# Layer A's channel-major products: high and low half of the input as one 512-column operand, and their sums joined ahead of the convolution

## The chip, the cores and the metric

The kernel runs on one core of one Trainium2 chip, in one launch. The metric is the device time of that launch in microseconds, as the median of several runs. Before the change it is 1284.6 us, the median of 3 runs from 1283.5 to 1285.86.

## What is computed

The reference is a decoder trunk of two layers on 256 rows of 2048 channels, in float32. Only layer A matters here. Its mixer multiplies the modulated input `h` by one wide weight matrix, and puts a causal convolution of width 4 along the sequence on the part that holds x, B and C:

```python
h = x * (1.0 + scale) + shift
proj = h @ in_w
z, xBC, dt = jnp.split(proj, [SSD_D_INNER, SSD_D_INNER + SSD_CONV_DIM], axis=-1)
xBC = jax.nn.silu(_causal_depthwise_conv(xBC, conv_w, conv_b))
xs, Bm, Cm = jnp.split(xBC, [SSD_D_INNER, SSD_D_INNER + SSD_BC_DIM], axis=-1)
...
y = _ssd_chunked(xs * dt[..., None], dt * A, Bm, Cm)
...
y = y * jax.nn.silu(z.astype(jnp.float32))
```

A gated norm, an output product, a layer norm, keys and values for all of layer B, and layer B's windowed attention follow.

## The kernel before

**Products in halves.** Each float32 operand of a large product is split into a high half, which float32r holds, and a low half, the rest. A product of two such operands takes three matmuls: high by high, high by low, low by high. The weights come from HBM in pieces of 128 partitions x 1024 float32 (512 KB; `load_piece`, L86, six buffers `raw`), and `split` (L91) makes `whi` on ACT (L94) and `wlo` on DVE (L95, raw minus whi), four buffers each. The input's halves of layer A lie in `hp` (L269): all 16 blocks of the high half, then all 16 of the low half, 256 columns a block. In layer B they lie in `xp` (L702), and there the high and low half of one block are neighbours.

**Two forms of a channel-major product.** In such a product the weights are what TensorE holds, and the input streams past; the result has channels on partitions and the 256 rows as columns. `cm_piece` (L109) issues, for each of 2 blocks of the input and each of 4 blocks of 128 output channels, three matmuls of 256 columns: L119 (`hi` by `ahi`), L120 (`hi` by `alo`) and L121 (`lo` by `ahi`), all into one half of a PSUM bank. `cm_quad` (L133) does a whole product of 512 channels so. `cm_wide` (L140), used in layer B alone, does 256 channels: one matmul of 512 columns (L151: `hi` by both halves of the input, which fills a bank with two sums side by side) and one of 256 (L152: `lo` by `ahi`, onto the first half of the bank). Its two sums are joined behind it by an ACT copy (L156) and a DVE add (L157). Its pieces hold 4 input blocks x 256 channels, where those of `cm_quad` hold 2 blocks x 512 channels; both are 512 KB.

**Layer A.** The program has a head (L351 to L490), in which the input is modulated as its column products arrive, and in which 10 later products are begun with the blocks that are there (`begun`, L292: the part sums lie in `szt` and in `y[0..7]` until needed). Then `product` (L326) is called for each group: `xs` of groups 1 to 7 and `bc` (B and C of two groups) of 2, 4 and 6 are channel-major; `z` is not. Of the channel-major ones `xs` 1 and `bc` 2 have blocks 4 to 15 left (`k0=4`), `bc` 4 and `bc` 6 blocks 12 to 15 (`k0=12`), and the other six all 16. `product` takes `cm_quad`'s two banks as four tiles (`tiles`, L159). Where a part sum exists, two DVE adds of 512 columns put the banks onto it (L344). The convolution (`conv`, L298) then reads each tile four times: an ACT activation (L302) and three DVE operations of 255, 254 and 253 columns (L305), and ACT's SiLU ends it (L307). It reads PSUM where there was no part sum, SBUF where there was one.

**What shares the engines there.** Between the products stand the scores and the scan of each group (`stage1`, `stage2`, `stage3`), and one column product of the gate, a DVE pass over 2048 columns (L236), goes with every fifth piece (`R = (1, 5)`). PSUM has eight banks; in this stage four are `mm` (tiles `acc`), two `aux`, two `aux2`. A pair of `acc` takes two of the four.

**What sets the order.** Nothing is run as it is written: `arrange` (L1316) lists all instructions with their dependencies, prices each (`price`), runs a list scheduling of the whole program six times and fixes the order of every engine's queue by the best. So an edit in one stage can move instructions in another.

Of the kernel before, what the change touches and what calls it, by code (L numbers as in the profile page):

```python
# [19 lines left out]
P = 128  # L20
# [23 lines left out]

CI, CT, CM, NCONST = 0, 128, 256, 512

CD, CA, NBIAS = 0, 256, 256 + 768


@with_exitstack  # L50
def trunk(ctx, tc, xT, x, c, par, cst, bias, lnrow, ada, wdt, win, wout, wkv, wk1, wbin, wbout, out):
    nc = tc.nc
    V, S, T, PO = nc.vector, nc.scalar, nc.tensor, nc.gpsimd

# [85 lines left out]
    def cm_wide(src, dst, rate=(0, 1)):  # L140


        ps = acc_pair()
        for q in range(KT // 4):
            hi, lo = (t.rearrange("p k n -> p (k n)").rearrange("p (k n) -> p k n", k=4)
                      for t in split(load_piece(src[q])))
            for k in range(4):
                kt = 4 * q + k
                for n in range(2):
                    c_ = slice(n * P, n * P + P)  # L150
                    T.matmul(ps[n], hi[:, k, c_], xp[:, kt], start=kt == 0, stop=False, skip_group_check=True)  # L151
                    T.matmul(ps[n][:, 0, :], lo[:, k, c_], xhi[:, kt, :], start=False, stop=kt == KT - 1,  # L152
                             skip_group_check=True)
            background(*rate)
        for n in range(2):
            S.activation(dst[:, n, :], ps[n][:, 1, :], AF.Copy)  # L156
            V.tensor_tensor(dst[:, n, :], ps[n][:, 0, :], dst[:, n, :], op=ALU.add)  # L157
# [108 lines left out]
            jobs.pop(0)()  # L266


    hp = act.tile([P, 2, KT, L], F32R, name="actT")  # L269
    hhi, hlo = hp[:, 0], hp[:, 1]  # L270

    with ExitStack() as cA:
        pa = cA.enter_context(tc.tile_pool(name="pa", bufs=1))
# [13 lines left out]
        with ExitStack() as cS:  # L287
# [38 lines left out]
            def product(kind, g, pre=None):  # L326

                src, k0, part = begun.get((kind, g), (None, 0, None))
                if src is None:
                    src = win[{"bc": g // 2, "xs": 4 + g, "z": 12 + g}[kind]]  # L330
                if kind == "z":
                    ps = tm_chunk(src, hh_, hl_, rate=R, k0=k0, pre=pre)
                    if g not in sz:
                        sz[g] = p0.tile([P, 2, 512], F32, name="sz")
                    for b in range(2):
                        if part is not None:
                            V.tensor_tensor(part[:, b, :], ps[b], part[:, b, :], op=ALU.add)
                        S.activation(sz[g][:, b, :], part[:, b, :] if part is not None else ps[b], AF.Silu)
                    return
                ps = cm_quad(src, hhi, hlo, rate=R, k0=k0)  # L340
                t = tiles(ps)
                if part is not None:
                    for w in range(2):
                        V.tensor_tensor(part[:, 2 * w:2 * w + 2, :], ps[w], part[:, 2 * w:2 * w + 2, :], op=ALU.add)  # L344
# [387 lines left out]
    with ExitStack() as cL:  # L732
        pl = cL.enter_context(tc.tile_pool(name="pl", bufs=3))
        ex = cL.enter_context(tc.tile_pool(name="ex1", bufs=2, space=PSUM))
        ps = [acc_pair(), acc_pair(), acc_pair(ex)]
        cm_quads([(wkv[2 * g], ps[g]) for g in range(NG)], xhi, xlo, pre=ahead)
        for g in range(NG):
            evict_k(0, g, ps[g])

        R = (4, 9)  # L740
        queue(pl, cols1[16:])
        jobs.append(lambda: gate_out(1))
        for g in range(NG):
            for w in range(2):
                cm_wide(wk1[2 * g + w], kk[1][:, g, 2 * w:2 * w + 2, :], rate=R)
# [32 lines left out]
    def queries(hq):  # L778
        qq = pc2.tile([P, 12, L], F32, name="qq").rearrange("p (g i) l -> p g i l", g=NG)
        for g in range(NG):  # L780
            for w in range(2):
                cm_wide(wbin[2 * (2 * g + hq) + w], qq[:, g, 2 * w:2 * w + 2, :])
        return qq

    def attend(hq, qq):
# [37 lines left out]
    def z_gate(hq, qq):  # L823
        for w in range(2):
            z = qq[:, 1, 2 * w:2 * w + 2, :]
            cm_wide(wbin[2 * (6 + hq) + w], z)
            S.activation(z, z, AF.Silu)
        V.tensor_tensor(qq[:, 0], qq[:, 0], qq[:, 1], op=ALU.mult)

# [525 lines left out]
def _layout(x, c, ada_w, ada_b, ln_g, ln_b, a_in_w, a_conv_w, a_conv_b, a_dt_bias,  # L1355
            a_A_log, a_D, a_norm_g, a_out_w, kv_w, b_in_w, b_out_w):
    f = np.float32
    par = np.zeros((P, NPAR), f)

    def put(name, a):  # L1360
        par[:a.shape[0], OFF[name][0]:OFF[name][1]] = a

    ab = ada_b.reshape(2, 3, KT, P)
    put("adab", ab.transpose(3, 0, 2, 1).reshape(P, 96))
    put("convw", a_conv_w[0].T.reshape(48, P, 4).transpose(1, 0, 2).reshape(P, 192))
    put("convb", _cm(a_conv_b[0]))
# [27 lines left out]
    return {  # L1394
        "xT": x[0].T.reshape(KT, P, L).transpose(1, 0, 2), "x": x[0], "c": c, "par": par, "cst": cst, "bias": bias,
        "lnrow": np.stack([ln_g[0], ln_b[0], ln_g[1], ln_b[1]]),
        "ada": ada, "wdt": _dt(dt), "win": win,
        "wout": _pieces(a_out_w[0]), "wkv": _pieces(kv_w), "wbin": _pieces(b_in_w[0], 256, 4),
        "wk1": _pieces(kv_w[:, :3072].reshape(D, 3, 2, 512)[:, :, 1].reshape(D, 1536), 256, 4), "wbout": _pieces(b_out_w[0]),
    }  # L1400
# [21 lines left out]
```

## Time and profile before

| | before |
|---|---|
| median of 3 runs | 1284.6 us (1283.5 to 1285.86) |
| the profiled execution, its own time | 1281.55 us |
| its span, first to last instruction | 1279.8 us |
| mean granted TensorE clock | 0.993 |
| PE busy | 1239.4 us, 97% |
| DVE busy | 1039.2 us, 81% |
| ACT busy | 696.6 us, 54% |
| read from HBM | 331.37 MB |

Matmuls are pipelined: the duration of one (about 285 ns for 256 columns) runs from its issue to its end and overlaps the next, so the sum over PE's groups is far more than its busy time. What a stream of matmuls costs is read from the spacing of their starts, in the timeline.

### The profile page before, as it was taken

What the parts mean: (1) busy time and instruction counts of PE and PEld (TensorE: products, weight loads), DVE (VectorE), ACT (ScalarE), POOL (GpSimd) and SP (SyncE); (2) the same over time, 40 slices, a digit from 0 to 9 for tenths busy, and PEclk for the clock granted to TensorE, in tenths of its full rate; (3) what the DMA queues carried; (4) which work ended last, traced back from release to release, by engine and by line L of the source; (5) the groups of instructions that cost most, each with busy time, mean ns of one, the idle gap of its engine ahead of it and who ended that gap; (6) DMA issues with size and microseconds to landing.
All of it is one profiled execution on the core that took longest, in us unless ns stands there. A gap on an engine that the chain in (4) does not pass through costs nothing.

```text
span 1279.8 us, 19378 instructions
## 1 busy us (share of the span) xinstructions
PE 1239.4 (97%) x7386; PEld 1095.2 (86%) x7386; DVE 1039.2 (81%) x1457; ACT 696.6 (54%) x1027; POOL 33.3 (3%) x20
## 2 busy tenths in 40 slices
PE   6999999999999999999999899999999999999995
PEld 4978999899899999788888699888888888888884
DVE  6999978999998887978895799998745647848778
ACT  4644566868577767764333444444445645444551
POOL 0000000000000000000000135000000000000000
PEclk9999999999999999999999899999999999999998
DMA  9999967887785556578997688999866663453571
GB/s 372 422 422 422 384 216 268 314 276 247 240 300 191 173 159 203 162 258 269 400 376 218 222 315 308 396 420 395 299 191 193 211 185 115 147 183 107 155 266 66
DMA packets 80449, 334.82 MB, mean 262 GB/s; under 512 B 9090, under 2 KB 9314, under 8 KB 67684
## 3 DMA queue, kind: packets, MB, share of 16 engines
q1 hardware_dynamic: 80356, 333.58, 73.5%
q8 instruction: 58, 0.95, 0.3%
q14 instruction: 35, 0.29, 0.1%
HBM read 331.37 MB, written 2.18 MB: 261 GB/s over the span
## 4 chain that ended last, share of the span: by engine, by line
PE 78%; DMA 12%; DVE 7%; ACT 1%; issue 1%; SPq 0%; DVEq 0%; ACTq 0%
PE acc L151 12%; PE acc L174 11%; PE acc L173 11%; PE acc L172 11%; PE acc L152 6%; DMA raw<-in_win 6%; PE acc L119 6%; PE acc L121 6%; PE acc L120 6%; DMA araw<-in_ada 5%; DVE wlo L95 2%; PE py L589 1%; DVE araw L236 1%; PE aux L795 1%; PE po L819 1%
## 5 line engine op out<-in xcount | busy, mean ns | idle before, releaser
L95 DVE TENSOR_TENSOR wlo<-raw,whi 128x1024 fp32r<-128x1024 f32 x395 | 488.9, 1244 | 176.5 <-ACT whi L94 175.2
L94 ACT ACTIVATE whi<-raw 128x1024 fp32r<-128x1024 f32 x395 | 417.1, 1057 | 382.1 <-PE acc L174 178.6
L119 PE MATMUL acc<-actT,whi 128*128 128x256 f32 x960 | 273.6, 288 | 11.8 <-ACT actT L382 7.4
L173 PE MATMUL acc<-wlo,actT 128*128 128x512 f32 x704 | 276.4, 393 | 0.6 <-DVE wlo L95 0.6
L172 PE MATMUL acc<-whi,actT 128*128 128x512 f32 x704 | 274.8, 393 | 1.6 <-ACT whi L94 1.0
L121 PE MATMUL acc<-actT,wlo 128*128 128x256 f32 x960 | 270.5, 285 | 1.4 <-DVE wlo L95 1.4
L120 PE MATMUL acc<-actT,whi 128*128 128x256 f32 x960 | 271.3, 285 | 0.0
L151 PE MATMUL acc<-actT,whi 128*128 128x512 f32 x704 | 251.3, 398 | 0.0
L236 DVE SCALAR_TENSOR_TENSOR araw<-araw,cb__72 128x2048 f32<-128x2048 f32 x96 | 218.4, 2286 | 9.0 <-DMA araw<-in_ada 5.7
L152 PE MATMUL acc<-actT,wlo 128*128 128x256 f32 x704 | 201.8, 287 | 0.6 <-DVE wlo L95 0.6
L119 PEld LDWEIGHTS acc<-actT,whi 128*128 128x128 f32 x960 | 185.2, 194 | 15.7 <-ACT actT L382 9.0
L121 PEld LDWEIGHTS acc<-actT,wlo 128*128 128x128 f32 x960 | 184.0, 193 | 2.3 <-DVE wlo L95 2.0
L120 PEld LDWEIGHTS acc<-actT,whi 128*128 128x128 f32 x960 | 185.1, 193 | 0.3
L174 PE MATMUL acc<-whi,actT 128*128 128x512 f32 x448 | 175.1, 391 | 0.0
L172 PEld LDWEIGHTS acc<-whi,actT 128*128 128x128 f32 x704 | 131.9, 188 | 30.1 <-ACT whi L94 2.8
L151 PEld LDWEIGHTS acc<-actT,whi 128*128 128x128 f32 x704 | 132.2, 188 | 29.2
L173 PEld LDWEIGHTS acc<-wlo,actT 128*128 128x128 f32 x704 | 132.3, 188 | 27.5 <-DVE wlo L95 1.1
L152 PEld LDWEIGHTS acc<-actT,wlo 128*128 128x128 f32 x704 | 133.0, 189 | 1.9 <-DVE wlo L95 1.2
L174 PE MATMUL acc<-whi,ylo 128*128 128x512 f32 x256 | 100.8, 394 | 0.0
L174 PEld LDWEIGHTS acc<-whi,actT 128*128 128x128 f32 x448 | 84.1, 188 | 17.5 <-issue 0.5
L174 PEld LDWEIGHTS acc<-whi,ylo 128*128 128x128 f32 x256 | 48.1, 188 | 9.4
L305 DVE SCALAR_TENSOR_TENSOR cacc<-acc,prm,cacc 128x255 f32<-128x255 f32 (+2 forms) x96 | 43.7, 475 | 2.7 <-ACT cacc L302 2.3
(205 smaller groups left out, 1083.1 us busy)
## 6 DMA issues: line engine op xcount, KB each, us to landing
araw<-in_ada SPq DMA_DIRECT2D x96, 1024.0 KB, 7.2
raw<-in_win SPq DMA_DIRECT2D x160, 512.0 KB, 4.9
raw<-in_wkv SPq DMA_DIRECT2D x72, 512.0 KB, 4.9
raw<-in_wout SPq DMA_DIRECT2D x64, 512.0 KB, 5.6
raw<-in_wbin SPq DMA_DIRECT2D x64, 512.0 KB, 4.0
raw<-in_wk SPq DMA_DIRECT2D x24, 512.0 KB, 6.6
cbc<-cumd SPq DMA_DIRECT2D x16, 512.0 KB, 5.3
raw<-in_wbout SPq DMA_DIRECT2D x16, 512.0 KB, 4.3
```

The lines of the kernel that those rows point to most:

```text
L94: S.activation(hi, raw, AF.Copy)
L95: V.tensor_tensor(lo, raw, hi.bitcast(F32), op=ALU.subtract)
L119: T.matmul(o, hi[:, k, c_], ahi[:, kt, :], start=first, stop=False, skip_group_check=True)
L120: T.matmul(o, hi[:, k, c_], alo[:, kt, :], start=False, stop=False, skip_group_check=True)
L121: T.matmul(o, lo[:, k, c_], ahi[:, kt, :], start=False, stop=kt == k1 - 1, skip_group_check=True)
L151: T.matmul(ps[n], hi[:, k, c_], xp[:, kt], start=kt == 0, stop=False, skip_group_check=True)
L152: T.matmul(ps[n][:, 0, :], lo[:, k, c_], xhi[:, kt, :], start=False, stop=kt == KT - 1, skip_group_check=True)
L172: T.matmul(ps[b], h_, hi[:, k, :], start=kt == k0, stop=False)
L173: T.matmul(ps[b], h_, lo[:, k, :], start=False, stop=False)
L174: T.matmul(ps[b], l_, hi[:, k, :], start=False, stop=kt == k1 - 1)
L236: V.scalar_tensor_tensor(raw, raw, 1.0, cb_, op0=ALU.mult, op1=ALU.mult, accum_out=mod[layer][:, ct, j:j + 1])
L305: V.scalar_tensor_tensor(acc[:, o:], ps[:, :L - o], w[:, j:j + 1], acc[:, o:], op0=ALU.mult, op1=ALU.add)
```

## The change

The input's halves of layer A are laid out as those of layer B, block by block (`hp` becomes blocks x 2 halves x 256). `cm_quad` goes away. `cm_wide` takes its operands as arguments and a first block `k0`, and returns its banks; what stood behind it, the copy and the add of layer B, becomes `cm_join`, which layer B's calls now use. `product` does each of its ten channel-major products as two `cm_wide` of 256 channels, from pieces of a new input `wsub`, which holds the same weights cut as layer B's are (4 blocks x 256 channels). Behind each half, two tiles are made: without a part sum, an ACT copy of the bank's second half into a new SBUF tile `ct` and a DVE add of its first half; with one, two DVE adds of 256 columns onto the part sum. The convolution reads SBUF in every case but group 0, which the head computes as before; `cm_piece` is left to the head and to layer B's first three products.

```diff
-    def cm_quad(src, ahi, alo, rate=(0, 1), k0=0):
+    def cm_wide(src, both, high, rate=(0, 1), k0=0):
+
         ps = acc_pair()
-        for q in range(k0 // 2, KT // 2):
-            cm_piece(src, q, ps, ahi, alo, k0=k0)
-            background(*rate)
-        return ps
...
+        for q in range(k0 // 4, KT // 4):
             hi, lo = (t.rearrange("p k n -> p (k n)").rearrange("p (k n) -> p k n", k=4)
                       for t in split(load_piece(src[q])))
             for k in range(4):
                 kt = 4 * q + k
                 for n in range(2):
                     c_ = slice(n * P, n * P + P)
-                    T.matmul(ps[n], hi[:, k, c_], xp[:, kt], start=kt == 0, stop=False, skip_group_check=True)
-                    T.matmul(ps[n][:, 0, :], lo[:, k, c_], xhi[:, kt, :], start=False, stop=kt == KT - 1,
+                    T.matmul(ps[n], hi[:, k, c_], both[:, kt], start=kt == k0, stop=False, skip_group_check=True)
+                    T.matmul(ps[n][:, 0, :], lo[:, k, c_], high[:, kt, :], start=False, stop=kt == KT - 1,
                              skip_group_check=True)
             background(*rate)
+        return ps
...
-    hp = act.tile([P, 2, KT, L], F32R, name="actT")
-    hhi, hlo = hp[:, 0], hp[:, 1]
+    hp = act.tile([P, KT, 2, L], F32R, name="actT")
+    hhi, hlo = hp[:, :, 0, :], hp[:, :, 1, :]
...
-                ps = cm_quad(src, hhi, hlo, rate=R, k0=k0)
-                t = tiles(ps)
-                if part is not None:
-                    for w in range(2):
-                        V.tensor_tensor(part[:, 2 * w:2 * w + 2, :], ps[w], part[:, 2 * w:2 * w + 2, :], op=ALU.add)
-                    t = [part[:, n, :] for n in range(4)]
+                t = []
+                for w in range(2):
+                    ps = cm_wide(wsub[2 * WSUB.index((kind, g)) + w], hp, hhi, rate=R, k0=k0)
+                    for n in range(2):
+                        if part is None:
+                            t.append(p0.tile([P, L], F32, name="ct", bufs=4))
+                            S.activation(t[-1], ps[n][:, 1, :], AF.Copy)
+                            V.tensor_tensor(t[-1], ps[n][:, 0, :], t[-1], op=ALU.add)
+                        else:
+                            t.append(part[:, 2 * w + n, :])
+                            for i in range(2):
+                                V.tensor_tensor(t[-1], ps[n][:, i, :], t[-1], op=ALU.add)
```

TensorE's queue at the start of the product `xs` of group 2, before (`acc_2673` and `acc_2674` are its two banks):

```order
L119 MATMUL acc_2673<-actT_86,whi_2677 128x256
L120 MATMUL acc_2673<-actT_86,whi_2677 128x256
L121 MATMUL acc_2673<-actT_86,wlo_2678 128x256
L119 MATMUL acc_2674<-actT_86,whi_2677 128x256
L120 MATMUL acc_2674<-actT_86,whi_2677 128x256
```

(The second block of 128 channels, in the same bank as the first, stands between the third and the fourth row.) The same product after the change, where its first half (`acc_2593`, `acc_2594`) ends and its second begins; L145 and L146 are the two matmuls of the new `cm_wide`:

```order
L145 MATMUL acc_2593<-actT_86,whi_2666 128x512
L146 MATMUL acc_2593<-actT_86,wlo_2667 128x256
L145 MATMUL acc_2594<-actT_86,whi_2666 128x512
L146 MATMUL acc_2594<-actT_86,wlo_2667 128x256
L145 MATMUL acc_2692<-actT_86,whi_2696 128x512
L146 MATMUL acc_2692<-actT_86,wlo_2697 128x256
```

Three matmuls of 256 columns became one of 512 and one of 256; a bank now holds one block of 128 channels where it held two, and a product uses two pairs of banks one after the other.

DVE's queue behind the first half of that product, after the change (L345 joins the sums in `ct`, L303 is the convolution, L97 makes a `wlo`):

```order
L97 TENSOR_TENSOR wlo_2766<-raw_2763,whi_2765 128x1024
L345 TENSOR_TENSOR ct_2686<-acc_2593,ct_2686 128x256
L345 TENSOR_TENSOR ct_2689<-acc_2594,ct_2689 128x256
L97 TENSOR_TENSOR wlo_2872<-raw_2869,whi_2871 128x1024
L303 SCALAR_TENSOR_TENSOR cacc_2792<-ct_2686,prm_74,cacc_2792 128x255
L303 SCALAR_TENSOR_TENSOR cacc_2798<-ct_2689,prm_74,cacc_2798 128x255
L303 SCALAR_TENSOR_TENSOR cacc_2792<-ct_2686,prm_74,cacc_2792 128x254
L303 SCALAR_TENSOR_TENSOR cacc_2798<-ct_2689,prm_74,cacc_2798 128x254
L97 TENSOR_TENSOR wlo_2942<-raw_2939,whi_2941 128x1024
```

Before, no L345 stood there, and the convolution's operations read `acc_2673` itself:

```order
L95 TENSOR_TENSOR wlo_3102<-raw_3099,whi_3101 128x1024
L305 SCALAR_TENSOR_TENSOR cacc_2922<-acc_2673,prm_74,cacc_2922 128x255
L213 SCALAR_TENSOR_TENSOR ay_2435<-at_2439,ay_2435 128x2
L305 SCALAR_TENSOR_TENSOR cacc_2922<-acc_2673,prm_74,cacc_2922 128x254
L537 TENSOR_TENSOR cb_2951<-aux_2948,cc_75 128x256
L305 SCALAR_TENSOR_TENSOR cacc_2922<-acc_2673,prm_74,cacc_2922 128x253
```

Two adds moved in between splits of later weights, and the convolution was moved behind them.

The place with the shortest halves is `bc` of group 4, where one piece is left to each half. DVE's queue there after the change (`acc_3408` and `acc_3409` are the first half's banks, `acc_3436` and `acc_3437` the second's; L594 is a group's scan, `wlo_3520` belongs to the `xs` product behind):

```order
L594 TENSOR_TENSOR y2_92<-py_3380,y2_92 128x512
L97 TENSOR_TENSOR wlo_3520<-raw_3517,whi_3519 128x1024
L349 TENSOR_TENSOR y3_93<-acc_3408,y3_93 128x256
L349 TENSOR_TENSOR y3_93<-acc_3409,y3_93 128x256
L349 TENSOR_TENSOR y3_93<-acc_3408,y3_93 128x256
L349 TENSOR_TENSOR y3_93<-acc_3409,y3_93 128x256
L97 TENSOR_TENSOR wlo_3542<-raw_3539,whi_3541 128x1024
L349 TENSOR_TENSOR y3_93<-acc_3436,y3_93 128x256
```

The same product before (line numbers of before; `acc_3588` and `acc_3589` are its banks, and L594 and L213 belong to a norm):

```order
L95 TENSOR_TENSOR wlo_3776<-raw_3773,whi_3775 128x1024
L344 TENSOR_TENSOR y3_93<-acc_3588,y3_93 128x512
L594 TENSOR_SCALAR ms_3572<-ss_3543 128x2
L213 SCALAR_TENSOR_TENSOR ay_3053<-at_3057,ay_3053 128x2
L95 TENSOR_TENSOR wlo_3806<-raw_3803,whi_3805 128x1024
L344 TENSOR_TENSOR y3_93<-acc_3589,y3_93 128x512
```

Four adds now empty the first half's pair, where two of 512 columns emptied the whole product. On TensorE the second half's 16 matmuls stand between the last one into `acc_3409` and the first of the next product, which needs the two banks that these adds free.

More of the change, by code (lines that the diff above doesn't have):

```diff
@@ L45, with trunk @@
 CI, CT, CM, NCONST = 0, 128, 256, 512
+WSUB = [("xs", g) for g in range(1, G)] + [("bc", g) for g in (2, 4, 6)]
 CD, CA, NBIAS = 0, 256, 256 + 768
 @with_exitstack
-def trunk(ctx, tc, xT, x, c, par, cst, bias, lnrow, ada, wdt, win, wout, wkv, wk1, wbin, wbout, out):
+def trunk(ctx, tc, xT, x, c, par, cst, bias, lnrow, ada, wdt, win, wsub, wout, wkv, wk1, wbin, wbout, out):
     nc = tc.nc
@@ L131, in acc_pair @@
         return [(pool or mm).tile([P, 2, L], F32, name="acc") for _ in range(2)]
-    def cm_quad(src, ahi, alo, rate=(0, 1), k0=0):
+    def cm_wide(src, both, high, rate=(0, 1), k0=0):
         ps = acc_pair()
-        for q in range(k0 // 2, KT // 2):
-            cm_piece(src, q, ps, ahi, alo, k0=k0)
-            background(*rate)
-        return ps
-    def cm_wide(src, dst, rate=(0, 1)):
-        ps = acc_pair()
-        for q in range(KT // 4):
+        for q in range(k0 // 4, KT // 4):
             hi, lo = (t.rearrange("p k n -> p (k n)").rearrange("p (k n) -> p k n", k=4)
@@ L150, in cm_wide, with cm_join @@
                     c_ = slice(n * P, n * P + P)
-                    T.matmul(ps[n], hi[:, k, c_], xp[:, kt], start=kt == 0, stop=False, skip_group_check=True)
-                    T.matmul(ps[n][:, 0, :], lo[:, k, c_], xhi[:, kt, :], start=False, stop=kt == KT - 1,
+                    T.matmul(ps[n], hi[:, k, c_], both[:, kt], start=kt == k0, stop=False, skip_group_check=True)
+                    T.matmul(ps[n][:, 0, :], lo[:, k, c_], high[:, kt, :], start=False, stop=kt == KT - 1,
                              skip_group_check=True)
             background(*rate)
+        return ps
+    def cm_join(src, dst, rate=(0, 1)):
+        ps = cm_wide(src, xp, xhi, rate)
         for n in range(2):
@@ L744, in trunk @@
             for w in range(2):
-                cm_wide(wk1[2 * g + w], kk[1][:, g, 2 * w:2 * w + 2, :], rate=R)
+                cm_join(wk1[2 * g + w], kk[1][:, g, 2 * w:2 * w + 2, :], rate=R)
         for hq in range(2):
@@ L781, in queries @@
             for w in range(2):
-                cm_wide(wbin[2 * (2 * g + hq) + w], qq[:, g, 2 * w:2 * w + 2, :])
+                cm_join(wbin[2 * (2 * g + hq) + w], qq[:, g, 2 * w:2 * w + 2, :])
         return qq
@@ L825, in z_gate @@
             z = qq[:, 1, 2 * w:2 * w + 2, :]
-            cm_wide(wbin[2 * (6 + hq) + w], z)
+            cm_join(wbin[2 * (6 + hq) + w], z)
             S.activation(z, z, AF.Silu)
@@ L1397, in _layout @@
         "ada": ada, "wdt": _dt(dt), "win": win,
+        "wsub": _pieces(np.concatenate([xs[:, 512:], bc[:, 512:]], 1), 256, 4),
         "wout": _pieces(a_out_w[0]), "wkv": _pieces(kv_w), "wbin": _pieces(b_in_w[0], 256, 4),
```

## The prediction, on record before the result

> **What bounds the kernel now.** I read the page's first part, then who waits on PE, then the stages by windows, then the timeline of single matmuls. First the page's busy times and the chain that ended last:
>
> ```profile
> PE 1239.4 (97%) x7386; PEld 1095.2 (86%) x7386; DVE 1039.2 (81%) x1457; ACT 696.6 (54%) x1027; POOL 33.3 (3%) x20
> PE 78%; DMA 12%; DVE 7%; ACT 1%; issue 1%; SPq 0%; DVEq 0%; ACTq 0%
> ```
>
> PE is busy 97% of the span and holds 78% of the chain. What it waits for, longest first in the list of waits (who, for whom, us in total, times, longest):
>
> ```profile
> PE acc L119 <- ACT actT L382: 7.4, 1, 7.4
> PE aux L711 <- ACT u L696: 5.7, 1, 5.7
> PE acc L119 <- ACT whi L94: 3.9, 5, 2.0
> ...
> PE acc L121 <- DVE wlo L95: 1.4, 3, 0.6
> ```
>
> The first is the start of the program, the second the layer norm. Neither is touched. The ten products that change are issued from about 180 us to 500 us. So I asked for that stage, for its densest stretch of DVE, and for two later stretches (per stretch: length, busy us and count of PE, weight load, DVE, ACT, POOL, then granted clock, DMA share, GB/s):
>
> ```profile
> 165.00:530.00 365.00, 363.91 (x2524) 336.96 (x2523) 321.40 (x510) 265.79 (x443) 0.00 (x0) 1.00 0.69 231
> 240.00:400.00 160.00, 159.58 (x1135) 149.24 (x1134) 148.67 (x230) 113.45 (x186) 0.00 (x0) 1.00 0.76 258
> ...
> 600.00:640.00 40.00, 40.00 (x178) 33.11 (x177) 35.71 (x34) 15.45 (x15) 0.00 (x0) 1.00 1.01 400
> ...
> 840.00:880.00 40.00, 40.00 (x221) 34.75 (x220) 37.42 (x40) 17.12 (x21) 0.00 (x0) 1.00 1.02 413
> ```
>
> In the stage PE idles 365 - 363.91 = 1.1 us, at full clock. DVE is next with 321.4 of 365 us, 88.1%, and ACT has 265.8; DMA at 0.69 is no limit. The stage is bound by PE's stream, so what counts is how fast PE issues, not how long a matmul lasts.
>
> **The change, part by part.**
>
> *The matmuls.* Spacing of starts, from the timeline (start, duration): the first and last of 51 steps of the old triple in the stage, of 36 steps of the wide pair that layer B has already, and of 27 steps of matmuls of 512 columns in the output product.
>
> ```profile
> 300.04 0.28 PE L119 MATMUL acc<-actT,whi 128*128 128x256 f32 x1
> ...
> 306.15 0.28 PE L119 MATMUL acc<-actT,whi 128*128 128x256 f32 x1
> ...
> 859.63 0.39 PE L151 MATMUL acc<-actT,whi 128*128 128x512 f32 x1
> ...
> 865.87 0.39 PE L151 MATMUL acc<-actT,whi 128*128 128x512 f32 x1
> ...
> 619.75 0.39 PE L173 MATMUL acc<-wlo,actT 128*128 128x512 f32 x1
> ...
> 625.87 0.39 PE L173 MATMUL acc<-wlo,actT 128*128 128x512 f32 x1
> ```
>
> Triple: 6.11 / 17 = 359.4 ns, or 119.8 ns a matmul. Pair: 6.24 / 18 = 346.7 ns. A lone 512: 6.12 / 27 = 226.7 ns. So the durations mislead: three of 0.28 against 0.39 + 0.28 would promise 170 ns a block, but the starts give **12.7 ns**.
>
> How many blocks: six whole products of 16 x 4, two of 12 x 4 (`xs` 1, `bc` 2), two of 4 x 4 (`bc` 4, `bc` 6): 384 + 96 + 32 = 512. PE gains 512 x 12.7 ns = **6.5 us**.
>
> The Trainium skill, in "TensorE: Matmul & The Clock Gate", section "Back-to-back issue gap", prices a warm isolated matmul at its columns over 2.4 GHz plus about 2.5 ns; by that a triple would be 327.5 ns and a pair 325.0, and the sum a gain of 1.3 us in place of 6.5. The rows here are above it for both forms (119.8 against its 109.2, 226.7 against 215.8), so by this trace the fixed part of a matmul is larger, and dropping one is worth more.
>
> *The joining.* The prices, from a grouping of layer B's L157 and L156, and from the groups within 165 to 530 us (count | busy us, mean ns | idle before):
>
> ```profile
> L157 DVE TENSOR_TENSOR qq<-acc,qq 128x256 f32<-128x256 f32 x32 | 13.4, 420 | 8.1 <-ACT qq L156 8.1
> ...
> L156 ACT ACTIVATE qq<-acc 128x256 f32<-128x256 f32 x32 | 12.0, 379 | 21.0 <-PE acc L152 21.0
> ...
> L95 DVE TENSOR_TENSOR wlo<-raw,whi 128x1024 fp32r<-128x1024 f32 x111 | 134.4, 1222 | 35.1 <-ACT whi L94 34.4
> L305 DVE SCALAR_TENSOR_TENSOR cacc<-acc,prm,cacc 128x255 f32<-128x255 f32 (+2 forms) x96 | 43.7, 475 | 2.7 <-ACT cacc L302 2.3
> L305 DVE SCALAR_TENSOR_TENSOR cacc<-y,prm,cacc 128x255 f32<-128x255 f32 (+2 forms) x48 | 20.9, 476 | 0.0
> L344 DVE TENSOR_TENSOR y<-acc,y 128x512 f32<-128x512 f32 x8 | 5.4, 685 | 0.6 <-PE acc L121 0.6
> ...
> L94 ACT ACTIVATE whi<-raw 128x1024 fp32r<-128x1024 f32 x113 | 118.6, 1053 | 58.9 <-PE acc L174 33.4 <-PE acc L120 21.6 <-issue 1.7
> ...
> L302 ACT ACTIVATE cacc<-acc,prm 128x256 f32<-128x256 f32 x32 | 17.3, 558 | 17.2 <-DVE cacc L305 9.2 <-PE acc L121 7.9
> L302 ACT ACTIVATE cacc<-y,prm 128x256 f32<-128x256 f32 x16 | 8.9, 588 | 0.0
> ```
>
> DVE gains 24 adds (six products, four tiles) and 32 (four products with a part sum, four tiles, two adds), and loses the 8 of L344: 56 x 0.420 - 8 x 0.685 = **+18.0 us**. The convolution costs the same from SBUF (476 against 475 ns). ACT gains 24 copies of 0.379 = 9.1 us, and 24 x 30 ns where L302 now reads SBUF: +9.8 us.
>
> What hides it: DVE would need 321.4 + 18.0 = 339.4 us of a stage of 365 - 6.5 = 358.5, or 94.7%; ACT 275.6, or 77%. If nothing hid it, the 18 us would stand on the path. I take it as hidden, at nothing, because most of DVE's idle time is slack and not need: 35.1 of its 43.6 us lie ahead of `wlo` and wait for ACT's `whi`, and ACT's own idle ahead of `whi` ends with PE (33.4 and 21.6 us), which gives a weight buffer back. DVE waits because PE is full.
>
> *The new waits.* A DVE add waits for the last matmul of its half and, without a part sum, for the ACT copy; the queue behind it then holds the splits of weights, for which PE waits. In the order shown, two adds stand between `wlo_2766` and `wlo_2872`: 0.84 us, against four buffers of `wlo`, each worth 8 blocks x 346.7 ns = 2.77 us of PE. The banks: a half of a whole product takes PE 32 x 346.7 ns = 11.1 us, and its pair is emptied in about 1.6 us (2 x 0.379 + 2 x 0.420). At `bc` 4 and `bc` 6 a half is only 2.77 us, and four adds take 1.68; 1.1 us are left, if DVE is there in time. I take nothing, with 1.7 us a half as the other end.
>
> *At nothing for a plain reason.* The pieces of `wsub` are as many (64) and as large as those they replace, in a layout that the trace has: a median of 4.9 us to landing for `in_win`, 4.0 and 6.6 for the two inputs cut so:
>
> ```profile
> raw<-in_win SPq DMA_DIRECT2D x160, 512.0 KB, 4.9
> ...
> raw<-in_wbin SPq DMA_DIRECT2D x64, 512.0 KB, 4.0
> raw<-in_wk SPq DMA_DIRECT2D x24, 512.0 KB, 6.6
> ```
>
> SP's queue has them in PE's order, and at 0.69 DMA has room for 6.6. The new layout of `hp` leaves each matmul's columns adjacent. The head computes as before; its order is only redrawn in places.
>
> *Does the gain reach the end?* Behind the stage PE is full too: 40.00 of 40 us in the two stretches quoted last, even where DMA is at 1.01 and 1.02. There a transfer waits for a buffer that PE's progress frees, so it starts earlier with it. I carry the 6.5 us through whole.
>
> *Sum.* The profiled execution took 1281.55 us for a span of 1279.8; 6.5 less gives 1275.0. Beside the median of 1284.6, which is 3.05 above that execution, it gives **1278.1 us**.
>
> **The rivals.**
>
> *DVE becomes the bound (slower).* The place is DVE's queue in the stage, where the adds stand ahead of `wlo`. For it: 88.1% before, 94.7% needed. The point at which it decides is the share that DVE can hold: at 93.0% (339.4 / 365) the gain is gone, below it the kernel is slower. The densest 160 us had 148.67, or 92.9%, but those were not at a limit, since PE lost only 0.4 us there. At 88.1%, as the stage was, it lasts 385.4 us and the kernel is 20.4 slower: 1305. Half way, at 90.5%, it lasts 375.0: +10.0, **1294.6**. Chance 0.17.
>
> *The hand-over of banks eats it (no change).* Twenty halves at 1.7 us would be 34 us, but 16 of them have 8 to 11 us of PE work to hide it. Four are short; if all are bare, 4 x 1.7 = 6.8, and the time is 1284.6 - 6.5 + 6.8 = **1284.9**. Against it: PE's 1.1 us of idle time in the whole stage leaves no room for a matmul that waited for a bank, and 1.1 us were left above. Chance 0.09.
>
> *The wide form saves nothing: only columns count.* 768 columns are streamed either way. At the pace of the 512 rows, 0.443 ns a column, both forms cost 340 ns, and the time stays **1284.6**. Against it: triple and pair are measured above, in long streams. The page's rule named above is nearly this case. Chance 0.06.
>
> **How the numbers follow.** The forecast has 0.68. Its own range is 1274 to 1282: the 1.1 us that PE still idles in the stage and some 3 us of spread, that of the three runs, below; 4 us of redrawn order and short waits above. The full range, **1273 to 1290**, takes in both cases of no change and the milder half of the slow one; about 0.13 is left out. About 0.2%, or 2.6 us, is what a measurement of this kernel can tell from no change. Faster by more: 0.67. Within: 0.16. Slower by more: 0.17.
>
> **What would show it.** In the profile after: pairs 346.7 ns apart, 512 matmuls fewer, PE's idle time in the stage still near 1 us, and the output product begins 6 to 7 us sooner. DVE's share of the stage near 94%, its idle ahead of `wlo` down to some 20 us. It is wrong if PE waits for `wlo` (L97) or for an add (L345, L349) by several us in the stage, or if pairs are 359 ns apart. If the pace holds but the head before 165 us or the layer norm shifts by microseconds, the order redrawn elsewhere is the cause, and not this sum.

## The result, and the profile after

The changed kernel is slower. Its median is **1289.76 us** (20 runs, 1285.7 to 1292.43), against 1285.01 us for the kernel before (20 runs beside them): a ratio of **1.003, interval 1.002 to 1.004**. The forecast was 1278.1 us and faster. The profiled execution took 1289.58 us for a span of 1287.8, 8.0 more than the span of before. Two executions of the sessions below were disturbed, 3181.44 us of e6, which was its profiled one, and 2504.89 us of the kernel before; medians and ratios leave them out, and e9 is e6's kernel profiled again.

The page of the changed kernel: busy times, then the chain that ended last.

```profile
PE 1238.1 (96%) x6874; PEld 1066.8 (83%) x6874; DVE 1048.4 (81%) x1505; ACT 705.9 (55%) x1053; POOL 32.8 (3%) x20
...
PE 75%; DMA 12%; DVE 8%; issue 3%; ACT 1%; SPq 0%; DVEq 0%; ACTq 0%
```

512 matmuls are gone, and DVE and ACT are busy 9.2 and 9.3 us longer. But PE's share of the chain fell from 78% to 75%, while DVE and the engines' own issue gained. PE now waits more for `wlo`, in the third and fourth row of its list of waits:

```profile
PE acc L121 <- ACT actT L386: 10.4, 1, 10.4
PE aux L715 <- ACT u L700: 5.7, 1, 5.7
PE acc L123 <- DVE wlo L97: 5.4, 6, 2.4
PE acc L146 <- DVE wlo L97: 3.8, 6, 0.9
```

L123 and L146 are the matmuls that take the low half of the weights, and both wait for DVE's split. Before, the same two matmuls were L121, with 1.4 us, and L152:

```profile
PE acc L152 <- DVE wlo L95: 0.6, 2, 0.4
```

(The first row of after is the start of the program, where the list of before has 7.4 and 3.9 us in two rows.) To see where PE waits, I cut each kernel at two events that both have: the first transpose behind the layer norm (L711 before, L715 after), and the first product of layer B's attention (tile `po`). The first matmul of each is in these rows (count, shortest, median and longest in ns; start of the first and the last), of before, then of after:

```profile
L711 PE MATMUL aux<-cc,u x32: 270/272/476, 726.7 to 784.8; 128*128 128x128 f32 x32
...
L809 PE MATMUL po<-cc,sc x72: 270/272/329, 1076.8 to 1197.5; 128*128 128x128 f32 x72
```

```profile
L715 PE MATMUL aux<-cc,u x32: 270/272/476, 718.5 to 779.6; 128*128 128x128 f32 x32
...
L813 PE MATMUL po<-cc,sc x72: 270/272/328, 1082.8 to 1202.3; 128*128 128x128 f32 x72
```

Up to the layer norm the changed kernel **gains 8.2 us** (726.7 to 718.5). From there to the attention it takes 364.3 us in place of 350.1, so it **loses 14.2**; the rest takes 205.0 in place of 203.0, 2.0 more. The sum is 8.0. The edit touches nothing between norm and attention except that two calls were renamed: from the norm on both programs have the same 4131 instructions. Only their order differs.

The first 171.5 us behind the norm and what follows up to the attention, by windows, of before and of after (length, then busy us and count of PE, weight load, DVE, ACT, POOL; clock, DMA share, GB/s):

```profile
726.70:898.20 171.50, 169.80 (x1112) 155.87 (x1113) 163.36 (x168) 79.52 (x100) 33.08 (x16) 0.99 0.94 362
898.20:1076.80 178.60, 178.60 (x886) 150.88 (x885) 105.83 (x132) 90.13 (x120) 0.00 (x0) 1.00 0.66 206
```

```profile
718.50:890.00 171.50, 160.39 (x1052) 144.72 (x1053) 162.87 (x167) 72.89 (x93) 32.59 (x16) 0.99 0.95 357
890.00:1082.80 192.80, 192.70 (x947) 162.11 (x946) 108.41 (x133) 97.15 (x127) 0.00 (x0) 1.00 0.63 198
```

In the first 171.5 us PE gets 60 matmuls less done (1052 against 1112) and idles 11.1 us instead of 1.7; 8.9 of the 11.1 are waits for `wlo`. The 60 are matmuls of 512 columns: the timeline has 252 of them there in place of 312. At 226.7 ns each, the pace that the prediction read from L173, they are 13.6 us. They are done in the second stretch, which is full in both kernels (192.70 of 192.80) and 14.2 us longer. So the 14.2 us arise in the first stretch. That only 9.4 of them show as idle time there is probably because the record of a matmul runs on into the next, so that part of a pause counts as busy. DVE is the engine to look at: it holds 95% there in both.

### The profile page after: what moved, and what is told of

Read it like the earlier page. It is cut to its first block, busy times and chain, and to the rows that moved or that the text cites. A ratio compares the mean times of both kernels' runs of the same rounds, so it can differ in the third digit from the quotient of the medians.

```text
span 1287.8 us, 18441 instructions
## 1 busy us (share of the span) xinstructions
PE 1238.1 (96%) x6874; PEld 1066.8 (83%) x6874; DVE 1048.4 (81%) x1505; ACT 705.9 (55%) x1053; POOL 32.8 (3%) x20
## 3 DMA queue, kind: packets, MB, share of 16 engines
q1 hardware_dynamic: 80356, 333.58, 73.5%
## 4 chain that ended last, share of the span: by engine, by line
PE 75%; DMA 12%; DVE 8%; issue 3%; ACT 1%; SPq 0%; DVEq 0%; ACTq 0%
PE acc L145 18%; PE acc L171 12%; PE acc L172 12%; PE acc L170 12%; PE acc L146 9%; DMA raw<-in_win 6%; DMA araw<-in_ada 5%; DVE wlo L97 3%; DVE araw L234 3%; PE py L593 2%; PE acc L121 2%; PE acc L123 2%; PE acc L122 2%; PE aux L799 1%; PE po L823 1%
## 5 line engine op out<-in xcount | busy, mean ns | idle before, releaser
L97 DVE TENSOR_TENSOR wlo<-raw,whi 128x1024 fp32r<-128x1024 f32 x395 | 485.7, 1238 | 176.5 <-ACT whi L96 175.5
L145 PE MATMUL acc<-actT,whi 128*128 128x512 f32 x1216 | 433.2, 399 | 0.0
L146 PE MATMUL acc<-actT,wlo 128*128 128x256 f32 x1216 | 345.2, 285 | 3.8 <-DVE wlo L97 3.8
L145 PEld LDWEIGHTS acc<-actT,whi 128*128 128x128 f32 x1216 | 228.3, 188 | 52.7
L234 DVE SCALAR_TENSOR_TENSOR araw<-araw,cb__72 128x2048 f32<-128x2048 f32 x96 | 222.2, 2320 | 17.1 <-DMA araw<-in_ada 13.3
L146 PEld LDWEIGHTS acc<-actT,wlo 128*128 128x128 f32 x1216 | 229.7, 189 | 6.6 <-DVE wlo L97 5.7
L121 PE MATMUL acc<-actT,whi 128*128 128x256 f32 x448 | 127.1, 289 | 11.5 <-ACT actT L386 10.4
L123 PE MATMUL acc<-actT,wlo 128*128 128x256 f32 x448 | 126.6, 286 | 5.5 <-DVE wlo L97 5.4
L122 PE MATMUL acc<-actT,whi 128*128 128x256 f32 x448 | 126.9, 287 | 1.4 <-DVE actT L720 1.4
L121 PEld LDWEIGHTS acc<-actT,whi 128*128 128x128 f32 x448 | 86.4, 196 | 14.2 <-ACT actT L386 12.0
L123 PEld LDWEIGHTS acc<-actT,wlo 128*128 128x128 f32 x448 | 85.9, 193 | 7.2 <-DVE wlo L97 7.1
L122 PEld LDWEIGHTS acc<-actT,whi 128*128 128x128 f32 x448 | 86.5, 194 | 2.1 <-DVE actT L720 1.8
L552 ACT ACTIVATE seg<-cbc,cumT 128x128 f32<-128x128 f32 x128 | 40.0, 388 | 6.0 <-PE py L593 3.6
```

The costliest lines, as they stand in the source:

```text
L97: V.tensor_tensor(lo, raw, hi.bitcast(F32), op=ALU.subtract)
L121: T.matmul(o, hi[:, k, c_], ahi[:, kt, :], start=first, stop=False, skip_group_check=True)
L122: T.matmul(o, hi[:, k, c_], alo[:, kt, :], start=False, stop=False, skip_group_check=True)
L123: T.matmul(o, lo[:, k, c_], ahi[:, kt, :], start=False, stop=kt == k1 - 1, skip_group_check=True)
L145: T.matmul(ps[n], hi[:, k, c_], both[:, kt], start=kt == k0, stop=False, skip_group_check=True)
L146: T.matmul(ps[n][:, 0, :], lo[:, k, c_], high[:, kt, :], start=False, stop=kt == KT - 1, skip_group_check=True)
```

## The experiments

**What was open.** The scheduler takes the best of six rounds by its own estimate: for the kernel before its 4th, for the changed kernel its 2nd. In DVE's queue the last 32 column passes (`queue(pl, cols1[16:])`, 2048 columns each) stand among 61 splits in before and among 49 in after, so DVE meets them sooner. Theories: ORDER, the new order behind the norm makes DVE late there; LIMIT, the part behind the norm can't use an earlier start, whatever its order; PLACE, the new input moves the others in memory and the loads are slower. Later ORDER was divided: WORK (DVE has too much to do in the stretch) or LOADS (DVE's passes wait for column data, with splits queued behind them). All ratios are to the kernel before in the same session; differences in us are between medians, some of them of different sessions, unless the text says otherwise.

| run | median us (n) | ratio, 95% interval | norm to attention, us |
|---|---|---|---|
| before | 1285.01 (20) | 1 | 350.1 |
| after | 1289.76 (20) | 1.003 [1.002, 1.004] | 364.3 |
| e1_wide_old_tail | 1275.26 (6) | 0.9916 [0.9891, 0.9941] | 352.0 |
| e2_old_wide_tail | 1300.99 (6) | 1.0118 [1.0091, 1.0144] | 366.3 |
| e3_wide_round3 | 1278.83 (8) | 0.9947 [0.9928, 0.9966] | 353.0 |
| e10_old_round1 | 1301.14 (5) | 1.0141 [1.0118, 1.0163] | 364.0 |
| e4_unread_input | 1285.48 (10) | 1.0003 [0.9985, 1.0022] | 350.7 |
| e5_short_columns | 1275.11 (6) | 0.9917 [0.9898, 0.9936] | 350.2 |
| e6_small_loads | 1283.53 (11) | 0.9983 [0.9969, 0.9997] | 357.8 (of e9) |
| e7_old_tail_short_columns | 1273.55 (6) | 0.9906 [0.9885, 0.9927] | 349.1 |
| e8_short_pool | 1277.6 (12) | 0.9959 [0.9943, 0.9976] | 353.9 |

**e1 and e2: the two orders behind the norm, exchanged.** `retail` takes the last 4131 instructions (from the layer norm on) and refills each engine's places among them in the relative order that the other kernel has. e1 is the changed kernel with the tail's order of before, e2 the kernel before with that of after.

```diff
+    retail(best[1], P[0], len(work))
     last = {}
```

> The changed kernel; all instructions from the layer norm behind layer A on stand in each engine's queue in the relative order that they had before. Three theories. ORDER: the loss lies in the order that was redrawn behind the layer norm; with the old order there, layer A's gain of about 8 us (first transpose behind the norm at 712 us in place of 721) reaches the end: 1277 us, 1275 to 1279, a ratio of 0.992 to 0.995, and PE's waits for wlo between 712 and 900 us fall from about 15 us to about 2. LIMIT: the stage behind the norm is at its limit by DVE and DMA and cannot use an earlier start: 1284 to 1290, PE waits there as in the changed kernel. PLACE: reading the weights from a new, further input slows transfers (383 to 392 GB/s where 402 to 418 stood): 1288 to 1292.

> The kernel before; all instructions from the layer norm on stand in the relative order of the changed kernel. ORDER: it loses what the changed kernel lost there, 12 to 16 us: 1297 to 1301, with the norm still at about 721 us. LIMIT: no earlier start, so nothing collides: 1283 to 1288. PLACE: 1283 to 1287.

The order alone is worth 14.5 us in the changed kernel (1289.76 to 1275.26) and 16.0 in the one before (1284.98 to 1300.99); both times lie in ORDER's ranges. (The 712 and 721 us of the expectations are where PE's wait ahead of the norm's first transpose begins, 5.7 us before it. e2's profile has the norm at 731.9 us, 5.2 later than before, where no shift was expected: from 220 to 270 us its granted clock was 0.90, against 1.00 in before. The last column of the table starts at the norm and is free of this.) The stretch behind the norm in e1, from the same event on (its first transpose starts at 720.2):

```profile
720.20:891.70 171.50, 169.27 (x1104) 155.37 (x1105) 161.22 (x166) 78.76 (x100) 32.72 (x16) 0.98 0.94 357
```

1104 matmuls in place of 1052, and 2.2 us idle in place of 11.1, with the same instructions. ORDER holds. LIMIT falls: e1's tail starts 6.5 us sooner than that of before (720.2 against 726.7), and the attention starts 4.6 us sooner, so 1.9 of the 6.5 are lost on the way.

**e3 and e10: the scheduler's own rounds.** The changed kernel with its 4th round, and the kernel before with its 2nd: each kernel in the round that the other took.

```diff
-        if best is None or max(fin) < best[0]:
+        if k == 3:
```

(e10 has `k == 1`, on the kernel before.)

> The changed kernel with the order of the scheduler's fourth round in place of its second; the kernel before took its fourth. In that round the 32 column products behind the layer norm stand among the same 61 splits of weights as before; in the second they stand among 49. ORDER: as e1, 1275 to 1280, the last of the 32 columns at about 200 us behind the norm where it was 177. LIMIT: 1284 to 1290. PLACE: 1288 to 1292.

> The kernel before with the order of the scheduler's second round in place of its fourth, the round that the changed kernel took; its 32 columns behind the norm stand among 47 splits in place of 61. ORDER: slower by what the changed kernel lost by its round, 1289.8 - 1278.8 = 11 us or somewhat more: 1294 to 1302, so that the change is worth 6 to 11 us less in either round. If the round matters only together with the change: 1283 to 1288.

With the same round on both sides the change is a gain: in the 4th from 1284.98 to 1278.83, **6.2 us**, and in the 2nd from 1301.14 to 1289.76, 11.4 (14.3 by the ratios). In each kernel the 2nd round is the slower, by 10.9 us in the changed one and 16.7 in the one before. So the scheduler's estimate ranked the changed kernel's two rounds the wrong way round.

**e4: the new input alone.** The kernel before gets `wsub` as an input that nothing reads.

```diff
-def trunk(ctx, tc, xT, x, c, par, cst, bias, lnrow, ada, wdt, win, wout, wkv, wk1, wbin, wbout, out):
+def trunk(ctx, tc, xT, x, c, par, cst, bias, lnrow, ada, wdt, win, wsub, wout, wkv, wk1, wbin, wbout, out):
```

> The kernel before, with the new input wsub among its arguments and not read. ORDER and LIMIT: 1283 to 1287, a ratio of 1.000. PLACE: the other inputs move in HBM, several us slower, and under 395 GB/s between 800 and 880 us where 402 to 418 stood.

1.0003, with both sides of 1 in the interval. PLACE falls.

**e5 and e7: less DVE work in the passes, their loads unchanged.** In e5 the changed kernel's order is fixed as it was, in e7 as in e1; the last 32 column passes cover 256 of 2048 columns.

```diff
+    cut.append(1)
     queue(pl, cols1[16:])
...
-        V.scalar_tensor_tensor(raw, raw, 1.0, cb_, op0=ALU.mult, op1=ALU.mult,
+        d = slice(0, 256 if cut else D)
+        V.scalar_tensor_tensor(raw[:, d], raw[:, d], 1.0, cb_[:, d], op0=ALU.mult, op1=ALU.mult,
```

> The changed kernel with every queue in exactly its own order, but the DVE pass of the last 32 column products (those behind the layer norm) covers 256 of the 2048 columns; the rest of each is left out. Their loads stay as they are. That takes 32 x about 1.9 = 62 us off DVE behind the norm. Two theories of why the order is slow. WORK: 32 passes among 49 splits are more than DVE can do there, and the splits behind them come late. Then PE's waits for wlo between 712 and 900 us go from 15 us to under 3, and the time is that of e1 or less: 1270 to 1277. LOADS: the 32 loads of 1 MB stand too early in the DMA queue and hold up the weights and DVE, which waits for them with splits behind it. Then the time stays at 1285 to 1291.

> e1 (the changed kernel with the old order behind the norm), with the same cut of 32 DVE passes as in e5. WORK: in that order the passes fit, so little is won: 1271 to 1276, PE's waits behind the norm 1 to 2 us less than in e1; e5 and e7 come within 3 us of each other. LOADS: as e1, 1274 to 1277, and 9 us or more below e5.

e5's stretch behind the norm:

```profile
719.60:891.10 171.50, 170.93 (x1112) 156.88 (x1113) 114.61 (x176) 79.53 (x100) 24.82 (x16) 0.98 0.96 380
```

DVE falls from 162.87 to 114.61 us and PE is full, with the slow order. The time falls by 14.7 us to that of e1, into WORK's range. In the other order the same short passes bring only 1.7 (1275.26 to 1273.55), which lies within the two intervals. So what the slow order costs, it costs through these 32 passes. But a short pass also gives its buffer back sooner, so this does not yet tell WORK from LOADS.

**e6 and e9: smaller loads, the passes as long.** The last 32 column loads bring 128 KB in place of 1 MB, and the passes read 2048 columns of a constant tile. e9 is the same kernel, run once for its profile.

```diff
-        nc.sync.dma_start(raw, ada[layer, KIND.index(kind), ct])
+        d = slice(0, 256 if cut else D)
+        nc.sync.dma_start(raw[:, d], ada[layer, KIND.index(kind), ct][:, d])
...
-        V.scalar_tensor_tensor(raw, raw, 1.0, cb_, op0=ALU.mult, op1=ALU.mult,
+        V.scalar_tensor_tensor(raw, cb_ if cut else raw, 1.0, cb_, op0=ALU.mult, op1=ALU.mult,
```

> The changed kernel with every queue in exactly its own order, but the loads of the last 32 column products bring 256 of 2048 columns (128 KB in place of 1 MB), and their DVE passes, as long as before, read a constant tile in place of the load. WORK: nothing is gained, 1285 to 1291, PE's waits for wlo stay at 10 to 15 us. LOADS: the time is that of e1 or less, 1270 to 1277, and DVE's waits for column loads (8.6 us) vanish.

> e6 once more, for a profile: the changed kernel in its own order, the last 32 column loads 128 KB in place of 1 MB, the DVE passes as long as before on a constant tile. 1282 to 1286 by e6. If the loads matter only because DVE waits for them: DVE's waits for column loads (8.6 us) gone, PE's waits behind the norm down from about 15 to about 9 us. If they matter because weights come late: SP's and DVE's waits for whi change instead.

Now 1283.53 us: 6.2 less than after, which misses both ranges, that of WORK (no gain) and that of LOADS (the whole gain). What DVE waits for between 712 and 900 us, of after and then of e9 (L99 is the split there, L97 in after):

```profile
DVE araw L234 <- DMA araw<-in_ada: 8.6, 11, 1.2
DVE wlo L97 <- ACT whi L96: 2.0, 2, 1.5
```

```profile
DVE wlo L99 <- ACT whi L98: 8.2, 6, 1.5
DVE u L667 <- PE acc L174: 0.3, 1, 0.3
```

The waits for column data are gone, and PE's waits that are gone with them are those behind 800 us (L146 in after's list has no counterpart in e9's). Those ahead of 800 remain, as these three stretches of 20 us show, of after, then of e9:

```profile
732.00:752.00 20.00, 19.11 (x160) 18.90 (x160) 20.00 (x22) 9.04 (x12) 9.04 (x4) 1.00 0.97 359
752.00:772.00 20.00, 19.00 (x154) 18.22 (x153) 20.00 (x21) 8.18 (x10) 9.47 (x4) 1.00 0.87 321
772.00:792.00 20.00, 17.15 (x138) 16.49 (x137) 20.00 (x19) 6.21 (x7) 8.30 (x4) 1.00 0.90 310
```

```profile
732.00:752.00 20.00, 19.41 (x163) 19.20 (x162) 20.00 (x22) 9.99 (x13) 8.74 (x4) 1.00 0.60 183
752.00:772.00 20.00, 18.99 (x154) 18.21 (x153) 20.00 (x21) 8.34 (x11) 9.48 (x4) 1.00 0.60 191
772.00:792.00 20.00, 17.15 (x132) 16.48 (x131) 20.00 (x16) 6.21 (x7) 8.31 (x4) 0.95 0.49 160
```

DVE is busy 20.00 of 20 us in all six rows, even where DMA has fallen from 0.9 to 0.6, and PE idles 4.7 us in after and 4.5 in e9. There DVE waits for nothing; it has too much to do. So each theory holds in part, WORK ahead of 800 us and LOADS behind.

**e8: POOL's work beside DVE.** In those 60 us single DVE instructions are longer than usual, and always while POOL applies the layer norm's rows. e8 keeps the changed kernel's order and lets POOL's 16 operations behind the norm take 4 of 512 columns.

```diff
-                PO.tensor_tensor(u[b][:, cs_], u[b][:, cs_], lnr[0], op=ALU.mult)
-                PO.tensor_tensor(u[b][:, cs_], u[b][:, cs_], lnr[1], op=ALU.add)
+                few = slice(512 * n, 512 * n + 4)
+                PO.tensor_tensor(u[b][:, few], u[b][:, few], lnr[0][:, :4], op=ALU.mult)
+                PO.tensor_tensor(u[b][:, few], u[b][:, few], lnr[1][:, :4], op=ALU.add)
```

> The changed kernel with every queue in exactly its own order, but POOL's 16 operations on the residual behind the layer norm cover 4 of 512 columns; the rest of them is left out. In the changed kernel, as in the kernel before, 11 to 13 DVE operations between 724 and 796 us last about 1.09 us longer than their like, all while POOL works. WORK, with POOL's part: DVE gets some 12 us back in the stage where it is full (20.00 of 20 us from 732 to 792), no DVE operation is long any more, PE's waits for wlo before 800 us (8.7 us) all but vanish and those behind stay: 1279 to 1283. If the long operations have nothing to do with POOL: 1287 to 1292 and they stay.

1277.6 us: 12.2 less than after by the medians, 9.1 by the ratios (1.003 - 0.9959 of 1285), and below the range that was expected. DVE's groups between 700 and 900 us, of after and of e8 (count | busy us, mean ns of one):

```profile
L97 DVE TENSOR_TENSOR wlo<-raw,whi 128x1024 fp32r<-128x1024 f32 x62 | 81.3, 1323 | 8.0 <-ACT whi L96 8.0
L234 DVE SCALAR_TENSOR_TENSOR araw<-araw,cb__72 128x2048 f32<-128x2048 f32 x32 | 76.4, 2389 | 8.6 <-DMA araw<-in_ada 8.6
L720 DVE TENSOR_TENSOR actT<-xtmp,actT 128x256 fp32r<-128x256 f32 x16 | 9.0, 580 | 0.0
L719 DVE TENSOR_SCALAR xtmp<-aux,prm 128x256 f32<-128x256 f32 x16 | 8.0, 534 | 0.0
```

```profile
L99 DVE TENSOR_TENSOR wlo<-raw,whi 128x1024 fp32r<-128x1024 f32 x65 | 78.6, 1219 | 14.6 <-ACT whi L98 14.5
L236 DVE SCALAR_TENSOR_TENSOR araw<-araw,cb__72 128x2048 f32<-128x2048 f32 x32 | 73.2, 2289 | 10.1 <-DMA araw<-in_ada 9.8
L721 DVE TENSOR_SCALAR xtmp<-aux,prm 128x256 f32<-128x256 f32 x16 | 8.0, 537 | 0.0
L722 DVE TENSOR_TENSOR actT<-xtmp,actT 128x256 fp32r<-128x256 f32 x16 | 6.4, 414 | 0.0
```

One instruction on `wlo`, `araw` and `actT` is shorter by 104, 100 and 166 ns on the mean: 62 x 0.104 + 32 x 0.100 + 16 x 0.166 = 12.3 us less for DVE. In the three stretches where PE idled 4.7 us it idles no more; the middle one of e8:

```profile
752.00:772.00 20.00, 20.00 (x170) 20.00 (x169) 19.40 (x25) 8.68 (x12) 3.68 (x7) 1.00 1.00 398
```

Some waits behind 800 us remain, as LOADS has it (DVE still waits 9.8 us for `araw`). The two gains, 6.2 us and 9.1 to 12.2, are together as large as the 14.5 that the order is worth, or somewhat larger; how far they overlap the runs don't tell. Nor is e8's gain a part of what the order costs: POOL lengthens DVE's instructions in the kernel before too (13.4 us, see the last section), and there PE loses only 0.5 us in the same 60 us. What e8 shows is that DVE's time is what is short in those 60 us.

**What stays open.** e1 changes the order on all engines. That DVE's is the one that decides is inferred from e5 and e8, in which DVE gets less to do while every queue keeps its order; moving DVE's or SP's order alone, which would show it directly, wasn't tried. (With one queue exchanged alone, two queues could come to wait for each other; whether they would was not tried either.)

## Why the prediction was wrong, point by point

**What bounds the stage: right.** The same window of the stage in the changed kernel:

```profile
165.00:530.00 365.00, 363.66 (x2037) 312.91 (x2036) 340.48 (x577) 276.03 (x475) 0.00 (x0) 1.00 0.70 234
```

PE idles 1.3 us there (1.1 before).

**The joining, and what hides it: right that it is hidden; the size agrees in part by luck.** In this stretch DVE rose by 19.1 us (340.48 - 321.40; forecast 18.0) and ACT by 10.2 (forecast 9.8), and DVE holds 93.3% of it (forecast 94.7%). But the stretch has 67 more of DVE's records, where the edit adds 48, so other work moved in; over the whole program DVE is busy only 9.2 us longer. The price of one add was right: L345 and L349 have 418 and 417 ns on the mean (forecast 420). Added up, the durations of all of DVE's instructions are 17.8 us more; where one starts before the last has ended, busy time counts the overlap once, which the sum left out. PE doesn't pay for the adds. The rival in which DVE becomes the bound of this stage is out, though DVE is the bound elsewhere. The hand-over of the banks costs nothing that shows in 1.3 us.

**The matmuls: right in kind, too large in size.** The first and the last of 43 steps of the new pair in the stage:

```profile
299.42 0.40 PE L145 MATMUL acc<-actT,whi 128*128 128x512 f32 x1
...
314.61 0.40 PE L145 MATMUL acc<-actT,whi 128*128 128x512 f32 x1
```

15.19 / 43 = 353.3 ns, against 359.4 of the triple: 6.1 ns a block in place of 12.7, or 3.1 us in place of 6.5 for 512 blocks. Over all steps of the stage that are under 420 ns, the means are 359.2 and 350.5 ns: 8.6 ns a block, or 4.4 us. The 346.7 came from one place, around 860 us. The trace of before has another pace of the same pair, also in layer B; the first and the last of 191 steps:

```profile
1001.83 0.39 PE L151 MATMUL acc<-actT,whi 128*128 128x512 f32 x1
...
1069.30 0.40 PE L151 MATMUL acc<-actT,whi 128*128 128x512 f32 x1
```

67.47 / 191 = 353.2 ns. The prediction took the faster of the two; why a stretch has the one or the other is open. "Only columns count" is out: a gain is there.

**The gain at the norm: 8.2 us, and only part of it from the pairs.** The head (up to 165 us) did 27 matmuls more in the same time, 962 against 935, by its redrawn order; at 0.12 us each these are 3.2. In e3, whose head has 936 beside the 935 of before, the norm's first transpose stands at 721.3: 5.4 us sooner than before, which is the nearest to the forecast's 6.5. (In the other profiles with the changed kernel's order up to the norm it stands at 718.9 to 720.2, so 8.2 is the upper end.)

**"Does the gain reach the end?" is the step that failed.** It said that behind the stage PE is full too, and carried the 6.5 us through whole. Two things were wrong with it. PE full is no sign of slack in DVE: the stretches that I chose (600 to 640 and 840 to 880 us) had DVE at 35.71 and 37.42 of 40, and I left out the one between them, where both are full. This row of before was there to be read:

```profile
760.00:780.00 20.00, 20.00 (x170) 20.00 (x169) 20.00 (x21) 9.25 (x11) 8.79 (x4) 1.00 0.87 325
```

And I took the order behind the stage as given. I compared the queues at the place of the change alone, and put "4 us of redrawn order" into the range; the redrawn order costs 14.5 us (e1), more than twice the gain. Where DVE stands at 20.00 of 20 already, two more passes decide: the column passes in the first 73.5 us from the norm's first transpose, of before and of after (busy us and records, two records a pass):

```profile
726.70:800.20 73.50, 20.59 (x18) 0.97 0.86 307
```

```profile
718.50:792.00 73.50, 28.44 (x22) 0.97 0.90 318
```

Nine passes became eleven, and three of the eleven are lengthened by POOL, by 1.1 us each: 7.9 us more of DVE's time, while splits for PE stood behind. In the same 73.5 us DVE works on 20 splits in place of 22, and in the last 60 of them PE idles 4.7 us in place of 0.5.

The last line of the part on what would show it names the redrawn order as the cause if the head or the norm shifts by microseconds. It did not name the stretch behind the norm, and the case was given no price as a rival. A price could have been estimated from DVE's row above: at 100%, each pass of 2.3 us that moves into the stretch makes what stands behind it late by its whole length. For two passes that is 4.6 us, about what PE idles more in those 60 us; it is far from the whole 14.5.

## What to carry to other kernels

Where an order is redrawn by a scheduler, an edit has two effects, its own and that of the new order, and the second can be the larger: compare the queues over the whole program, above all where a second engine is at 100% beside the one that bounds, and price there what moved in. To measure the edit alone, hold the order (or the round) fixed on both sides: here 1.003 became 0.9947. The fastest kernel here that leaves nothing out is the changed one with the tail's order of before (e1): 1275.26 us, 0.9916.

## What the runs showed of the hardware that was not expected

While POOL (GpSimd) works, some DVE instructions are longer, most of them by 1.1 us: in these rows of the changed kernel's DVE timeline (start, duration) one pass takes 3.38 us and the next 2.28, one split 2.31 and another 1.21, an add 1.50 and the one before 0.41.

```profile
764.75 3.38 DVE L234 SCALAR_TENSOR_TENSOR araw<-araw,cb__72 128x2048 f32<-128x2048 f32 x1
...
772.08 2.28 DVE L234 SCALAR_TENSOR_TENSOR araw<-araw,cb__72 128x2048 f32<-128x2048 f32 x1
...
778.88 1.21 DVE L97 TENSOR_TENSOR wlo<-raw,whi 128x1024 fp32r<-128x1024 f32 x1
780.02 1.50 DVE L720 TENSOR_TENSOR actT<-xtmp,actT 128x256 fp32r<-128x256 f32 x1
781.44 2.31 DVE L97 TENSOR_TENSOR wlo<-raw,whi 128x1024 fp32r<-128x1024 f32 x1
```

In after 11 such instructions (11.9 us) belong to the three groups in the lists of e8 that read two operands from SBUF; e8 has none. The kernel before has 11 by 1.1 us and three of L716 by less, two of which stand here (0.94 and 0.93 in place of 0.42; the third is 0.74), together 13.4 us:

```profile
791.48 0.94 DVE L716 TENSOR_TENSOR actT<-xtmp,actT 128x256 fp32r<-128x256 f32 x1
...
795.15 0.93 DVE L716 TENSOR_TENSOR actT<-xtmp,actT 128x256 fp32r<-128x256 f32 x1
```

The fourth group in the lists of e8, `xtmp`, reads one operand from PSUM and has 534 and 537 ns. The Trainium skill, in "SBUF — State Buffer", section "Who interferes with whom", says that a DVE instruction with two SBUF inputs contends with a GpSimd instruction that reads SBUF, and that the later one blocks until the first is done. The trace agrees, in both directions. These two of POOL's operations in after (merged in the row) take 2.27 and 3.32 us:

```profile
763.71 5.56 POOL L771 TENSOR_TENSOR u<-u,lnr 128x512 f32<-128x512 f32 x2
```

The first, from 763.71, ends at 765.98, 1.15 us behind the split of L97 that runs from 762.51 to 764.83. The pass from 764.75, shown above, takes 1.1 us too long. POOL's second operation, from 765.94, ends at 769.27, again 1.14 us behind that pass. So the two take turns, and a DVE instruction that comes right behind another has nearly a whole operation of POOL ahead of it, which makes the addition the same 1.1 us so often. In the two rows of before, an `xtmp` operation, which does not wait, stands ahead of the add, and less of POOL's operation is left.

One group fits less well: two of the three L702 in after are longer by 0.97 us beside POOL, and those of before (L698), with POOL idle, are not. They read one operand of 512 columns and two of one column, so two wide operands are not needed; which of them collides the runs don't tell. The rows, of after and then of before:

```profile
L702 DVE TENSOR_SCALAR u<-u,m01y,m01nb 128x512 f32<-128x512 f32 x3 | 3.5, 1190 | 0.0
```

```profile
L698 DVE TENSOR_SCALAR u<-u,m01y,m01nb 128x512 f32<-128x512 f32 x3 | 1.6, 539 | 0.0
```
